# Six quads instead of four begin the MLP's first product with their plain products, and the activation sums are made in the order in which they are used

## The chip, the cores and the metric

The kernel runs on one core of one Trainium2 chip, as one launch. The metric is device microseconds of that core. Before the change the median of 3 runs is 2004.18 us (2002.26 to 2006.55). The engines are named as the profile names them: PE is TensorE's matmul, PEld its weight load, DVE is VectorE, ACT is ScalarE, POOL is GpSimd (it issues the stores), SP is SyncE (it issues the weight loads).

## The reference

Two layers of a decoder trunk on 1024 tokens of width 1024, in float32. Each layer is a mixer and then a squared-ReLU MLP, both with a norm ahead and a norm behind. Only the MLP matters here:

```
def squared_relu_mlp(h, w1, w2):
    return jnp.square(jax.nn.relu(h @ w1)) @ w2
...
        y = squared_relu_mlp(rms_norm(h, g[2]), ffn_w1[layer], ffn_w2[layer])
        h = h + rms_norm(y, g[3])
```

`w1` is 1024 x 4096 and `w2` is 4096 x 1024, for each of the two layers.

## The kernel before, in words

**Numbers.** Each float32 operand is split in a high and a low part: `split_slot` (L613) lets ACT cast to the high part (L614) and DVE subtract it from the source for the low part (L615). `mm3` issues three matmuls (L237 high by high, L238 high by low, L239 low by high).

**Quads.** The MLP's first product (`mlp_up`, L729) is cut into 16 quads of 256 hidden columns. A quad is a 2 x 2 block product (two halves of the contraction, two halves of the tokens) done with seven products instead of eight, on sums and differences of the blocks. Every product is 12 matmuls of 128x128 by 128x512 (`prod1`, L709). `plain(q)` makes two of them from the raw weights and raw activations (splits `b11`, `b21`): the first into bank pA, which ACT copies out as `p1` into half of the slot `x0` (L750), the second into bank pB, to which DVE adds `p1` (L755). Then come p6, p5, p7, p4, p3: p6 goes on accumulating on the first product in pA with `t2`, p5 starts bank pC with `t1`, p7 goes on in pA with `t3`, p4 in pA with `t4`, p3 in pC with `b22`. ACT copies pA to `u` after p6 and after p7 (`copy_u`, L737). Bank pA is held from `plain` to p4. There are eight banks.

**Operands of a quad.** `raw_w1` loads two 512 KB pieces r0 and r1 on SP (L604 is in `load`). `w1_plain` splits r0 for `plain`; `w1_sums` makes the weight sums va and vb with four DVE instructions (L653 to L656); `w1_split` splits them into w1hsa/w1sa (for p5 and p7) and w1hsb/w1sb (for p6 and p3); `w1_a22` splits half of r1 into w1x (for p4). The activations' sums are made once for each layer: `x_sums` (L685) makes t3, t1 and t2 (each two DVE subtractions of 128x1024, L693), splits t2, t1, t3, makes t4 and splits it, and splits b22 (each split two ACT casts and two DVE subtractions).

**Start of the stage.** When the first half of the tokens is ready, `plain(0)` to `plain(3)` run (EARLY = 4); for quads 1 to 3 r0 is loaded ahead into a slot of its own (`early_load`) and again with r1 later (`raw_w1`). When the second half is ready, `x_sums` is called as a whole, then `w1_split(0, "a")`, `w1_a22(0)`, and the rest of quad 0. The loop over q then does quad q's p4 and p3 and quad q+1's p6, p5 and p7; from quad 4 on it also does `plain(q+1)` ahead of p4(q), and p6(q+1) comes behind p3(q) instead of ahead of p4(q).

**Order.** The written order gives the priority; the order on each engine is fixed when the program is built, by priority among the instructions that are then reckoned to be ready. Each engine works through its list in that order. On-chip tiles come from 50 slots of 128x1024 float32 (`NSLOT`, `Slots`): `get` takes the slot that was freed longest ago, and a new tile waits for the last reader of the old one, which can be a store's landing. `sums(q)` makes the seven operands of the second product from quad q and stores them with POOL (L810, L811); their slots come back two to three products later in the written order.

Of the kernel before, what the change touches and what calls it, by code (L numbers as in the profile page):

```python
# [19 lines left out]
P = 128  # L20
# [129 lines left out]
class Trunk:  # L150
# [463 lines left out]
        self.nc.scalar.copy(hi, src)  # L614
        self.nc.vector.tensor_tensor(lo, src, hi.bitcast(F32), op=ALU.subtract)  # L615

    EARLY = 4

    def early(self, layer, step):

# [62 lines left out]
        return self.x_split([self.xr[dh, 0, j] for j in range(2)], True)  # L683

    def x_sums(self):  # L685
        tt = self.nc.vector.tensor_tensor
        b = {(dh, tg): [self.xr.pop((dh, tg, j)) for j in range(2)] for dh in range(2) for tg in range(2)}
        t1, t2, t4, b22 = b[0, 1], b[0, 0], b[1, 0], b[1, 1]
        t3 = [self.slots.get([P, 2, 512], F32, "t3") for _ in range(2)]

        def sub(d, x, y):
            for j in range(2):
                tt(d[j].t, x[j].t, y[j].t, op=ALU.subtract)  # L693
        sub(t3, b22, t1)
        sub(t1, t1, t2)
        sub(t2, b22, t1)
        self.xb["t2"] = self.x_split(t2, True)
        self.xb["t1"] = self.x_split(t1)
        self.xb["t3"] = self.x_split(t3)
        sub(t4, t4, t2)  # L700
        for s in t2:
            s.put()
        self.xb["t4"] = self.x_split(t4)
        self.xb["b22"] = self.x_split(b22)

    def mlp(self, layer, hsrc, hdst):
        self.mlp_up(layer).run(hsrc, hdst)
# [21 lines left out]
    def mlp_up(self, layer):  # L729
        nc, sl = self.nc, self.slots  # L730
        NQ, EARLY = 16, self.EARLY
        tt = nc.vector.tensor_tensor
        self.xb = {}
        Q = [dict() for _ in range(NQ)]

        def copy_u(q, j, bank):
            nc.scalar.copy(Q[q]["u"].t[:, j, :], bank.t)  # L737

        def relu2(ap, src):
            nc.scalar.activation(ap, src, AF.Relu)  # L740
            nc.scalar.activation(ap, ap, AF.Square)  # L741

        def plain(q):

            d = Q[q]
            d["A"] = self.hold("pA")
            d["x0"] = sl.get([P, 2, 512], F32, "hx0")
            c11, p1 = d["x0"].t[:, 0, :], d["x0"].t[:, 1, :]
            self.prod1(d["A"], q, "0", 0, "b11", True)
            nc.scalar.copy(p1, d["A"].t)  # L750
            b = self.hold("pB")
            self.prod1(b, q, "0", 1, "b21", True)
            for n in ("h0", "l0"):
                self.w1q[q][n].put()
            tt(c11, b.t, p1, op=ALU.add)  # L755
            b.put()
            relu2(c11, c11)

        def p6(q):
            Q[q]["u"] = sl.get([P, 2, 512], F32, "u")  # L760
            self.prod1(Q[q]["A"], q, "sb", 0, "t2", False)
            copy_u(q, 1, Q[q]["A"])

        def p5(q):
            Q[q]["C"] = self.hold("pC")
            self.prod1(Q[q]["C"], q, "sa", 1, "t1", True)

        def p7(q):
            d = Q[q]
            self.prod1(d["A"], q, "sa", 0, "t3", False)  # L770
            for n in ("sa", "hsa"):
                self.w1q[q][n].put()
            copy_u(q, 0, d["A"])
            d["x1"] = sl.get([P, 2, 512], F32, "hx1")
            c22 = d["x1"].t[:, 1, :]
            tt(c22, d["C"].t, d["u"].t[:, 0, :], op=ALU.add)
            relu2(c22, c22)

        def p4(q):
            d = Q[q]  # L780
            self.prod1(d["A"], q, "x", 0, "t4", False)
            self.w1q[q]["x"].put()
            relu2(d["x0"].t[:, 1, :], d["A"].t)
            d["A"].put()

        def p3(q):
            d = Q[q]
            self.prod1(d["C"], q, "sb", 1, "b22", False)
            for n in ("sb", "hsb"):
                self.w1q[q][n].put()  # L790
            c12 = d["x1"].t[:, 0, :]
            tt(c12, d["C"].t, d["u"].t[:, 1, :], op=ALU.add)  # L792
            d["C"].put()
            relu2(c12, c12)

        def sums(q):

            d = Q[q]
            g, r = q // 4, slice((q % 4) * 512, (q % 4) * 512 + 512)
            a11, a12 = d["x0"].t[:, 0, :], d["x0"].t[:, 1, :]  # L800
            a21, a22 = d["x1"].t[:, 0, :], d["x1"].t[:, 1, :]
            d["x2"] = sl.get([P, 2, 512], F32, "hx2")
            s1, s2 = d["x2"].t[:, 0, :], d["x2"].t[:, 1, :]
            tt(s1, a21, a22, op=ALU.add)
            tt(s2, s1, a11, op=ALU.subtract)
            tt(a21, a11, a21, op=ALU.subtract)
            tt(d["u"].t[:, 1, :], a12, s2, op=ALU.subtract)
            hs = self.hs[layer]
            for n, j in (("x0", 0), ("x1", 2), ("x2", 4)):
                nc.gpsimd.dma_start(hs[j:j + 2, g, :, r].rearrange("j p f -> p j f"), d[n].t)  # L810
            nc.gpsimd.dma_start(hs[6, g, :, r], d["u"].t[:, 1, :])  # L811
            self.later(8.0, lambda: [d[n].put() for n in ("x0", "x1", "x2", "u")])


        self.wait(lambda: self.xready[0] == [True, True])
        self.xb["b11"] = self.x_plain(0)
        self.xb["b21"] = self.x_plain(1)
        plain(0)
        self.early_load(layer, 2)
        self.early_load(layer, 3)  # L820
        plain(1)
        self.w1_sums(0)
        self.early_plain(2)
        plain(2)
        self.w1_split(0, "b")
        self.early_plain(3)
        plain(3)
        self.wait(lambda: self.xready[1] == [True, True])
        self.xready = [[False, False], [False, False]]
        self.gpost.put()  # L830
        self.x_sums()
        self.w1_split(0, "a")
        self.w1_a22(0)
        self.w1q[1]["raw"] = self.raw_w1(layer, 1)
        p6(0)
        p5(0)
        self.w1_sums(1)
        self.w1_split(1, "b")
        self.w1q[2]["raw"] = self.raw_w1(layer, 2)
        p7(0)  # L840
        down = None
        for q in range(NQ):
            n = q + 1
            if n < NQ:
                if n > 1:
                    self.w1_sums(n)
                if n >= EARLY:
                    plain(n)
                if n > 1:
                    self.w1_split(n, "b")  # L850
                if n < EARLY:
                    p6(n)
            else:
                down.step(4)
            p4(q)
            if n < NQ:
                self.w1_split(n, "a")
            else:
                down.step(4)
            p3(q)  # L860
            if n < NQ:
                if n >= EARLY:
                    p6(n)
                if n + 2 < NQ:
                    if "raw" not in self.w1q[n + 2]:
                        self.w1q[n + 2]["raw"] = self.raw_w1(layer, n + 2)
                self.w1_a22(n)
                p5(n)
                sums(q)
                if n + 1 < NQ and n + 1 >= EARLY:  # L870
                    self.w1_plain(n + 1)
                p7(n)
                if n == NQ - 2:
                    down = Down(self, layer)
                    down.load_w(0, 11)
                    down.load_h(0)
                if n == NQ - 1:
                    down.load_w(0, 22)
                    down.load_w(0, 12)
                    down.start()  # L880
                    down.load_h(1)
            else:
                sums(q)
        return down
# [343 lines left out]
class Down:  # L1228
# [29 lines left out]
    def tt(self, dst, a, b, op):  # L1258
        return [lambda j=j: self.k.nc.vector.tensor_tensor(dst[j].t, a[j].t, b[j].t, op=op) for j in range(2)]
# [254 lines left out]
```

## Time and profile before

| what | value |
|---|---|
| median of 3 runs | 2004.18 us |
| the profiled execution's own time | 2004.15 us |
| its span in the profile | 2002.4 us |
| granted TensorE clock, mean | 0.989 |
| busy: PE, PEld, DVE, ACT, POOL | 97%, 79%, 65%, 48%, 11% |
| bytes moved by DMA | 267.74 MB |

The profile's page gives busy time and share for each engine, the span in 40 slices, the DMA queues, the chain of work that ended last, groups of instructions and DMA issues. The timeline lists the instructions of one engine in order of time, each with its start, its duration and, in brackets, the idle time ahead of it and what ended that. Matmuls are pipelined, so a row's duration (0.39 us) is longer than the distance from one start to the next; distances between starts are what counts for PE.

### The profile page before, as it was taken

The page shows a single profiled execution, that of the slowest core. Times are in us where ns is not written, and L with a number is a line of the kernel's source. Part 1 is how long each engine was busy: PE and PEld are TensorE (multiplying, and loading weights), DVE is VectorE, ACT ScalarE, POOL GpSimd, SP SyncE. Part 2 cuts the span into 40 slices and gives each one's busy share as a digit, 9 for nine tenths or more (in the row PEclk, how much of TensorE's full clock was granted, in tenths as well). Part 3 has the DMA queues.
Part 4 walks back from the last instruction along what each step waited for, and adds up shares of the span by engine and source line. Part 5 has one row for each costly group of instructions (what it writes and reads, how often), then busy time and mean ns, then how long its engine had stood idle before and what let it go on. Part 6 is the DMA issues. An engine that isn't in the chain of part 4 may idle for free.

```text
span 2002.4 us, 23647 instructions
## 1 busy us (share of the span) xinstructions
PE 1948.1 (97%) x8836; PEld 1591.2 (79%) x8836; DVE 1310.5 (65%) x2023; ACT 965.0 (48%) x1612; POOL 216.2 (11%) x327
## 2 busy tenths in 40 slices
PE   8999989999999999989999999998999999999997
PEld 6888868788878888878778778786888887888886
DVE  5664486665584787993455556658665557578798
ACT  7223464555574433464344444656555556543342
POOL 3101101111110000051000001120111111000002
PEclk9999989999999999999999999999999999999999
DMA  8114226656684535452111113322555558453444
GB/s 295 40 64 137 79 90 174 153 147 163 166 264 154 167 119 167 157 182 69 43 43 43 32 32 106 121 90 84 169 156 158 153 166 260 149 176 127 150 134 168
DMA packets 76435, 267.74 MB, mean 134 GB/s; under 512 B 9157, under 2 KB 9157, under 8 KB 76320
## 3 DMA queue, kind: packets, MB, share of 16 engines
q1 hardware_dynamic: 48240, 168.84, 25.2%
q0 software_dynamic: 26784, 95.26, 16.4%
q10 hardware_dynamic: 1296, 2.13, 0.3%
q8 instruction: 69, 1.13, 0.2%
q14 instruction: 46, 0.38, 0.1%
HBM read 187.82 MB, written 78.38 MB: 133 GB/s over the span
## 4 chain that ended last, share of the span: by engine, by line
PE 83%; issue 10%; DVE 2%; DMA 2%; POOL 1%; ACT 1%; SPq 0%; POOLq 0%; DVEq 0%; ACTq 0%
PE p L237 10%; PE p L239 10%; PE p L238 10%; PE pA L237 4%; PE pA L239 4%; PE pA L238 4%; PE op L237 3%; PE op L239 3%; PE op L238 3%; PE pC L239 2%; PE pC L238 2%; PE pC L237 2%; PE pv L1188 1%; PE s L1121 1%; PE pB L239 1%
## 5 line engine op out<-in xcount | busy, mean ns | idle before, releaser
L238 PE MATMUL p<-wl,hh 128*128 128x512 f32 x896 | 348.5, 389 | 0.5 <-DVE wl L615 0.5
L239 PE MATMUL p<-wh,hl 128*128 128x512 f32 x896 | 348.7, 389 | 0.0
L237 PE MATMUL p<-wh,hh 128*128 128x512 f32 x896 | 347.6, 389 | 0.0
L238 PEld LDWEIGHTS p<-wl,hh 128*128 128x128 f32 x896 | 168.2, 188 | 35.8 <-DVE wl L615 0.9
L237 PEld LDWEIGHTS p<-wh,hh 128*128 128x128 f32 x896 | 168.2, 188 | 34.9
L239 PEld LDWEIGHTS p<-wh,hl 128*128 128x128 f32 x896 | 168.2, 188 | 34.9
L614 ACT CAST hh<-hr 128x1024 fp32r<-128x1024 f32 x112 | 115.2, 1052 | 123.5 <-PE p L239 41.2
L615 DVE TENSOR_TENSOR hl<-hr,hh 128x1024 fp32r<-128x1024 f32 x112 | 134.2, 1218 | 44.0 <-ACT hh L614 19.9
L1380 DVE TENSOR_TENSOR acc<-acc,p 128x512 f32<-128x512 f32 x168 | 114.4, 681 | 41.9 <-PE p L239 40.5
L810 POOL DMA_DIRECT2D hs<-hx x96 | 69.2, 722 | 568.5 <-ACT hx L741 417.3
L740 ACT ACTIVATE hx<-hx 128x512 f32<-128x512 f32 x96 | 60.6, 631 | 118.3 <-DVE hx L755 55.1
L614 ACT CAST wh<-w2r 128x1024 fp32r<-128x1024 f32 x64 | 67.0, 1053 | 95.4 <-PE p L238 90.3
L114 DVE TENSOR_TENSOR wlo<-raw,whi 128x1024 fp32r<-128x1024 f32 (+1 forms) x57 | 68.2, 1201 | 47.3 <-ACT whi L113 30.3
L615 DVE TENSOR_TENSOR wl<-w2r,wh 128x1024 fp32r<-128x1024 f32 x64 | 77.7, 1218 | 32.6 <-ACT wh L614 32.6
L1157 ACT ACTIVATE e<-s,nm 128x512 f32<-128x512 f32 (+3 forms) x96 | 54.6, 579 | 63.7 <-DVE nm L1150 54.0
L113 ACT CAST whi<-raw 128x1024 fp32r<-128x1024 f32 (+1 forms) x57 | 58.6, 1037 | 52.2 <-PE pp L239 15.8
L741 ACT ACTIVATE hx<-hx 128x512 f32<-128x512 f32 x128 | 80.9, 632 | 3.5
L614 ACT CAST wh<-t 128x1024 fp32r<-128x1024 f32 x48 | 50.1, 1050 | 56.5 <-PE p L238 52.2
L792 DVE TENSOR_TENSOR hx<-pC,u 128x512 f32<-128x512 f32 x32 | 22.0, 688 | 69.5 <-PE pC L239 69.5
L615 DVE TENSOR_TENSOR w1sb<-w1vb,w1hsb 128x1024 fp32r<-128x1024 f32 x32 | 39.1, 1223 | 41.9 <-PE pA L239 40.4
L239 PE MATMUL pC<-xb,w1sa 128*128 128x512 f32 x128 | 52.0, 407 | 14.3 <-DVE w1sa L615 14.3
L211 POOL DMA_DIRECT2D gain<-in_norm_g_dram x4 | 2.3, 573 | 577.2 <-PE p L239 476.2
(313 smaller groups left out, 4911.2 us busy)
## 6 DMA issues: line engine op xcount, KB each, us to landing
hr<-hs SPq DMA_DIRECT2D x112, 512.0 KB, 5.3
hs<-hx POOLq DMA_DIRECT2D x96, 512.0 KB, 4.7
w1r<-in_w_dram SPq DMA_DIRECT2D x70, 512.0 KB, 4.1
w2r<-in_w_dram SPq DMA_DIRECT2D x64, 512.0 KB, 5.5
h<-hd POOLq DMA_DIRECT2D x24, 512.0 KB, 4.8
hd<-y POOLq DMA_DIRECT2D x20, 512.0 KB, 3.0
hs<-u POOLq DMA_DIRECT2D x32, 256.0 KB, 7.5
rx<-in_xT_dram SPq DMA_DIRECT2D x16, 256.0 KB, 7.0
```

What stands on the lines that cost most here:

```text
L113: k.nc.scalar.copy(u.hi.t[:, f], u.raw.t[:, f])
L114: k.nc.vector.tensor_tensor(u.lo.t[:, f], u.raw.t[:, f], u.hi.t[:, f].bitcast(F32), op=ALU.subtract)
L237: mm(ps, ah, bh, start=start, stop=False, skip_group_check=more)
L238: mm(ps, ah, bl, start=False, stop=False, skip_group_check=more)
L239: mm(ps, al, bh, start=False, stop=stop, skip_group_check=more)
L614: self.nc.scalar.copy(hi, src)
L615: self.nc.vector.tensor_tensor(lo, src, hi.bitcast(F32), op=ALU.subtract)
L740: nc.scalar.activation(ap, src, AF.Relu)
L741: nc.scalar.activation(ap, ap, AF.Square)
L810: nc.gpsimd.dma_start(hs[j:j + 2, g, :, r].rearrange("j p f -> p j f"), d[n].t)
L1157: nc.scalar.activation(e[m][:, kb * 512:kb * 512 + n], banks[m, kb][:, :n], AF.Exp, scale=SCALE, bias=nm[:, m:m + 1], accum_out=sm[:, kb * ...
L1380: nc.vector.tensor_tensor(o, o, bank.t, op=ALU.add)
```

## The change

Six quads are early instead of four (`EARLY, HELD = 6, 4`). For quads 4 and 5 bank pA is given back after `p1` was copied out, and is filled again later by `refill`: one matmul into a new bank, whose result is then overwritten by an ACT copy of `p1` from `x0`, after which p6 accumulates on it. `refill(4)` stands in the loop at q = 2 and `refill(5)` at q = 3. `x_sums` becomes a generator with five stops: t2, t1 and t3 are split ahead of p6(0) and p5(0), interleaved with `w1_split(0, "a")`; t4 is made and split ahead of p4(0); b22 is split ahead of p3(0). `w1_a22(0)` moves behind p5(0). Quads 4 and 5 get early loads of r0 like quads 1 to 3.

```diff
-    EARLY = 4
+    EARLY, HELD = 6, 4
...
     def x_sums(self):
...
         self.xb["t2"] = self.x_split(t2, True)
+        yield
         self.xb["t1"] = self.x_split(t1)
+        yield
         self.xb["t3"] = self.x_split(t3)
+        yield
         sub(t4, t4, t2)
         for s in t2:
             s.put()
         self.xb["t4"] = self.x_split(t4)
+        yield
         self.xb["b22"] = self.x_split(b22)
+        yield
...
         def plain(q):
             d = Q[q]
-            d["A"] = self.hold("pA")
+            a = self.hold("pA")
             d["x0"] = sl.get([P, 2, 512], F32, "hx0")
             c11, p1 = d["x0"].t[:, 0, :], d["x0"].t[:, 1, :]
-            self.prod1(d["A"], q, "0", 0, "b11", True)
-            nc.scalar.copy(p1, d["A"].t)
+            self.prod1(a, q, "0", 0, "b11", True)
+            nc.scalar.copy(p1, a.t)
+            if EARLY > q >= self.HELD:
+                a.put()
+            else:
+                d["A"] = a
...
+        def refill(q):
+
+            d = Q[q]
+            d["A"] = self.hold("pA")
+            x = self.xb["b11"][0][0].t[:, 0, :]
+            nc.tensor.matmul(d["A"].t, x[:, :P], x, start=True, stop=True)
+            nc.scalar.copy(d["A"].t, d["x0"].t[:, 1, :])
...
-        self.early_plain(2)
-        plain(2)
-        self.w1_split(0, "b")
-        self.early_plain(3)
-        plain(3)
+        for q in range(2, EARLY):
+            self.early_plain(q)
+            plain(q)
+            if q == 2:
+                self.w1_split(0, "b")
+            if q + 2 < EARLY:
+                self.early_load(layer, q + 2)
         self.wait(lambda: self.xready[1] == [True, True])
...
-        self.x_sums()
+        xs = self.x_sums()
+        next(xs)
         self.w1_split(0, "a")
-        self.w1_a22(0)
+        next(xs)
         self.w1q[1]["raw"] = self.raw_w1(layer, 1)
         p6(0)
+        next(xs)
         p5(0)
+        self.w1_a22(0)
         self.w1_sums(1)
         self.w1_split(1, "b")
...
                 if n < EARLY:
                     p6(n)
+                if self.HELD <= n + 1 < EARLY:
+                    refill(n + 1)
+                if q == 0:
+                    next(xs)
...
             p4(q)
             if n < NQ:
                 self.w1_split(n, "a")
+                if q == 0:
+                    next(xs)
```

## Rows read from the trace of the kernel before

**Rows 1.** The page: busy time of PE, and the chain that ended last by engine.

```profile
PE 1948.1 (97%) x8836; PEld 1591.2 (79%) x8836; DVE 1310.5 (65%) x2023; ACT 965.0 (48%) x1612; POOL 216.2 (11%) x327
PE 83%; issue 10%; DVE 2%; DMA 2%; POOL 1%; ACT 1%; SPq 0%; POOLq 0%; DVEq 0%; ACTq 0%
```

**Rows 2.** The waits of PE over the whole span: who waited for whom, us in total, times, longest.

```profile
PE pC L239 <- DVE w1sa L615: 14.3, 2, 7.2
PE pA L237 <- ACT u L737: 9.6, 8, 2.5
...
PE pA L238 <- DVE xb L615: 3.2, 2, 1.6
```

**Rows 3.** The timeline of PE in layer 0, from the last matmul of `plain(3)` to the first of p4(0). The first of p6(1) starts at 296.26, the first of p4(0) at 298.98, twelve matmuls later.

```profile
274.84 0.39 PE L239 MATMUL pB<-xb,w1l 128*128 128x512 f32 x1
275.58 0.50 PE L237 MATMUL pA<-xb,w1hsb 128*128 128x512 f32 x1 [0.35 <-ACT xb L614]
...
278.13 0.50 PE L238 MATMUL pA<-xb,w1hsb 128*128 128x512 f32 x1 [1.58 <-DVE xb L615]
...
281.59 0.50 PE L237 MATMUL pA<-xb,w1hsa 128*128 128x512 f32 x1 [0.68 <-ACT u L737]
...
289.49 0.80 PE L239 MATMUL pC<-xb,w1sa 128*128 128x512 f32 x1 [7.16 <-DVE w1sa L615]
...
296.26 0.39 PE L237 MATMUL pA<-xb,w1hsb 128*128 128x512 f32 x1
...
298.98 0.39 PE L237 MATMUL pA<-xb,w1x 128*128 128x512 f32 x1
```

**Rows 4.** The same of layer 1: the last matmul of `plain(3)`, the end of the longest wait, the first matmul of p6(1).

```profile
1384.04 0.39 PE L239 MATMUL pB<-xb,w1l 128*128 128x512 f32 x1
...
1398.22 0.80 PE L239 MATMUL pC<-xb,w1sa 128*128 128x512 f32 x1 [7.17 <-DVE w1sa L615]
...
1405.28 0.39 PE L237 MATMUL pA<-xb,w1hsb 128*128 128x512 f32 x1
```

**Rows 5.** Windows of 5 us in layer 0: busy time of PE, PEld, DVE, ACT and POOL, then the granted TensorE clock, the mean busy share of the DMA engines and GB/s.

```profile
275.00:280.00 5.00, 3.07 (x13) 2.06 (x12) 5.00 (x6) 3.24 (x5) 0.00 (x0) 1.00 0.35 108
280.00:285.00 5.00, 1.65 (x7) 0.71 (x5) 5.00 (x6) 2.68 (x3) 0.00 (x0) 0.87 0.00 0
285.00:290.00 5.00, 0.51 (x1) 0.50 (x2) 5.00 (x6) 0.00 (x0) 0.00 (x0) 0.50 0.53 146
290.00:295.00 5.00, 5.00 (x15) 3.87 (x14) 4.96 (x8) 2.09 (x2) 0.00 (x0) 0.60 0.44 159
...
310.00:315.00 5.00, 4.98 (x23) 3.75 (x22) 3.72 (x6) 3.73 (x6) 0.42 (x1) 1.00 1.03 224
```

**Rows 6.** The timeline of DVE in layer 0, from the gap ahead of the activation sums to w1x of quad 0; a row can merge several instructions of one kind (x2, x4).

```profile
262.70 0.69 DVE L755 TENSOR_TENSOR hx<-pB,hx 128x512 f32<-128x512 f32 x1 [2.63 <-ACT hx L750]
...
266.59 2.35 DVE L693 TENSOR_TENSOR t<-xr,xr 128x1024 f32<-128x1024 f32 x2
268.86 2.35 DVE L693 TENSOR_TENSOR xr<-xr,xr 128x1024 f32<-128x1024 f32 x2
271.13 0.68 DVE L755 TENSOR_TENSOR hx<-pB,hx 128x512 f32<-128x512 f32 x1
271.73 2.35 DVE L693 TENSOR_TENSOR xr<-xr,xr 128x1024 f32<-128x1024 f32 x2
274.00 2.35 DVE L615 TENSOR_TENSOR xb<-xr,xb 128x1024 fp32r<-128x1024 f32 x2
...
276.87 2.35 DVE L615 TENSOR_TENSOR xb<-xr,xb 128x1024 fp32r<-128x1024 f32 x2
279.13 2.35 DVE L615 TENSOR_TENSOR xb<-t,xb 128x1024 fp32r<-128x1024 f32 x2
281.40 2.35 DVE L693 TENSOR_TENSOR xr<-xr,xr 128x1024 f32<-128x1024 f32 x2
283.68 4.62 DVE L615 TENSOR_TENSOR xb<-xr,xb 128x1024 fp32r<-128x1024 f32 x4
288.22 1.22 DVE L615 TENSOR_TENSOR w1sa<-w1va,w1hsa 128x1024 fp32r<-128x1024 f32 x1
289.35 0.68 DVE L615 TENSOR_TENSOR w1x<-w1r,w1x 128x512 fp32r<-128x512 f32 x1
```

**Rows 7.** ACT: the copy of pA to `u` after p6(0) and a cast of a weight sum, from the timeline; then, of the instructions on `hx` over the whole span, the copies from PSUM to SBUF (L750) and the squares from SBUF to SBUF (L741): count, ns min/median/max, first and last start.

```profile
280.95 0.59 ACT L737 COPY u<-pA 128x512 f32<-128x512 f32 x1 [2.68 <-PE pA L239]
291.27 1.04 ACT L614 CAST w1hsa<-w1va 128x1024 fp32r<-128x1024 f32 x1 [6.44 <-DVE w1va L656]
...
L741 ACT ACTIVATE hx<-hx x128: 615/632/637, 261.6 to 1689.3; 128x512 f32<-128x512 f32 x128
...
L750 ACT COPY hx<-pA x32: 561/589/590, 254.5 to 1660.9; 128x512 f32<-128x512 f32 x32
```

**Rows 8.** DMA: the issues of the w1 loads by the page (KB each, median us to landing), and the landing of the seven stores of `u` between 240 and 420 us.

```profile
w1r<-in_w_dram SPq DMA_DIRECT2D x70, 512.0 KB, 4.1
...
DMA to landing us min/median/max: 6.8/7.7/8.4
```

**Rows 9.** The waits of DVE over the whole span: the low split of the early weights waiting for a store of `u` to land (us in total, times, longest).

```profile
DVE w1l L615 <- DMA hs<-u: 19.3, 18, 4.1
```

**Rows 10.** The timeline of PE: the first matmul of p7(4) in layer 0.

```profile
356.08 0.50 PE L237 MATMUL pA<-xb,w1hsa 128*128 128x512 f32 x1 [2.05 <-ACT u L737]
```

## Prediction

> **What bounds the kernel.** I read the page first: PE is busy 97% of the span and PE rows make 83% of the chain that ended last [rows 1]. So only what takes time from PE counts, and the next view is PE's own waits. The longest by far is a product on pC that waits for w1sa of DVE, twice, 7.2 us at most [rows 2]: once for each layer, at the place that the change touches. The third view is PE's timeline there. In layer 0 the last matmul of plain(3) starts at 274.84; twelve matmuls take 2.72 us (296.26 to 298.98), so one takes 0.227 and the next product could have started at 275.07 [rows 3]. The first of p6(1) starts at 296.26. Between them lie p6(0), p5(0) and p7(0), 36 matmuls or 8.16 us; 296.26 - 275.07 - 8.16 = 13.03 us are lost. In layer 1 it is 1384.27 to 1405.28, so 12.85 us [rows 4]. Together **25.88 us**, 1.3% of the run.
>
> What ends these waits is read from DVE's timeline [rows 6]. From 266.59 DVE has no gap: t3, t1 and t2 are made, and then all the splits of t1, t2, t3, t4 and b22 until 288.2, and only then the low half of w1sa(0) at 288.22, for which p5(0) stands 7.16 us [rows 3]. t4 and b22, 6.8 us of DVE (281.40 to 288.22), are needed only by p4(0) and p3(0), two and three products later. A part of the loss is the clock: 20 matmuls lie between 289.49 and 296.26 and take 6.77 us where 4.53 is normal, so 2.24 us; the granted clock is 0.50 in the window with the long wait and 0.60 in the next, which is the lower level of 1.2 GHz mixed with the upper of 2.4 [rows 3, 5].
>
> **The change, part by part.**
>
> Plain products of quads 4 and 5. They go from the loop to the place of the wait: 48 matmuls, 10.88 us, so p6(0) comes at 285.95, not 275.07, in layer 0. PE's sum stays the same. What now must be ready, and when (one product is 2.72): t2 at 285.95, t1 and w1sa(0) at 288.7, t3 at 291.4, w1sb(1) at 294.1, t4 and w1x(0) at 296.8, b22 at 299.6.
>
> DVE up to p4(0), from the starts in [rows 6] (1.135 for 128x1024, 0.60 for 128x512): three sums 6.81; L755 of quads 2 to 5, 2.40; splits of t2, t1, t3, 6.81; w1sa(0) 1.13; w1x(0) 0.60; the four sums for quad 1, 2.40; w1sb(1) 1.13; t4 made and split 4.54; the combine at p7(0) 0.60; the two low splits for plain(4) and (5), 2.27 if they don't fit into the gap of 2.63 ahead of 262.70. Sum 28.7, so DVE is through at 295.3 where 296.8 is asked; b22 and w1sa(1) make 298.7 where 299.6 is asked. Within this t2 ends before 280 and w1sa(0) and t1 before 283. So the wait for w1sa(0) goes altogether; the margin at p4(0) is 1.5 us and thin. I take 25.88 us as the gain, since with it also the low clock goes; the lower bound comes below.
>
> Loads. Two more of 512 KB per layer, on SP ahead of raw_w1(1), in slots whose readers are matmuls of the output projection, over when plain(0) begins. A load lands after 4.1 us [rows 8], and plain(4) starts at 275.07: hidden. raw_w1(1) waits behind them and for slots that plain(2) frees 5.44 us (plain(3)) before 275.07; its sums are needed some 15 us later. If that cover went, each load would cost its 4.1.
>
> ACT. The casts for plain(4) and (5), their copies of pA and their squares move ahead with them; ACT stood idle for 6.44 us there, until 291.27 [rows 7], so they cost nothing.
>
> refill. Four matmuls in all on PE: 0.227 each, 0.91; the first matmul after a pause has rows of 0.50 [rows 3], so at most 2. Four ACT copies from SBUF to PSUM, a form that the trace lacks: between 0.56 (a copy the other way, L750) and 0.64 (a square in SBUF, L741) [rows 7]; I take 0.63. The copy has four products, 10.9 us, until p6 needs it. Hidden; without the cover 0.63 plus its wait, as after 281.59, about 1.
>
> Slots. I followed the gets and puts of the code. Two x0 slots more are held, so the fewest free falls from two to none at p4(1). The old tile under a new one is then often a very recent one: w1hsb(2) and w1sb(2) get the slots of w1sa(1) and w1hsa(1), which p7(1) reads until just before p6(2); w1sb(3) gets that of w1sa(2), read until p7(2) ends. So p6(2) can't follow p7(1) at once. Either p4(1) goes first, after the copy of pA to `u`, for which [rows 3] show a loss of 0.83 and a slow second matmul, 0.94; or PE stands for the cast and the low split, 1.04 + 1.22 + 0.3 = 2.6 less two matmuls, about 2.1. I take 0.94, as ACT has the copy first in written order. p6(3) waits for the low split after two matmuls: 1.22 + 0.2 - 0.45, about 1.0 (0 if p4(2) fills it). For p6(5) the sums come into slots of quad 2's stores: u(2) lands 6.8 to 8.4 us after its issue [rows 8], and then two sums, a cast and a split, 4.0 us, end about when p6(5) is due: 0 to 2, I take 0.5. Together 2.44 per layer, **4.9**.
>
> POOL. Stores of quads 2 to 4 come at the spacing of a quad without plain products (five products, 13.6 us) instead of 19.0. That means two loads of 512 KB and seven stores of 256 KB, 2.75 MB, in 13.6 us, 202 GB/s; the DMA engines are full in one window of this kind even now [rows 5]. No instruction is added on POOL.
>
> The wait of 2.05 us ahead of p7(4) [rows 10] belongs to the first quad with the late order. That is now quad 6; I count neither gain nor loss, and a gain of 0 to 2 as its bounds.
>
> Sum: -25.88 + 0.91 + 4.9 = -20.1. The profiled execution took 2004.15, so **1984.1 us**; the median is 2004.18, so nothing is added for that. With the best ends: 25.88 - 0.91 - 1.9 (p6(2) alone) + 2 = 25.1, or 1979. With the worst: 25.88 - 2 - 2 x (2.1 + 1.2 + 2) = 13.3, or 1991.
>
> **A rule against it.** The window with the wait of 1.58 us was granted 1.00, the next, with the 0.68 and the first part of the 7.16, 0.87, and only the one with the rest of the long wait 0.50 [rows 3, 5]. If each of the three new short waits per layer brought a stretch of low clock like the one seen (2.24), that would be 13.4 us and the run 1997.5. The Trainium skill, "TensorE: Matmul & The Clock Gate", section "A second HAM failure mode: psum-queue depth-cycling", says that pauses between groups of matmuls as banks are cycled are enough to make the clock swing; the rows here speak against it for waits of this length.
>
> **Rivals.**
>
> 1. The wait moves on: DVE's order still puts b22 or w1sa(1) ahead of t4, or p4(0) and p3(0) find their parts late. For it: 1.5 us of margin, and an order in which DVE took t1's split before t2's (the split of 274.00 did not release p6(0), that of 276.87 did [rows 3, 6]). Against it: t4 and b22 now stand later in written order. Price 2 to 8 us per layer, say 5: 1994. Chance 0.12.
> 2. Slower, by stores. With no slot free, DVE and ACT stand in order behind a landing of `u` in each of quads 2 to 5, where no plain product covers them. Such a wait exists now, 4.1 us at the longest, 19.3 in 18 [rows 9]. If PE lost 4.1 in all four quads of both layers, 33 us: 1984.1 + 33 = 2017. It decides from 3 us per quad on ((20.1 + 4) / 8). Against it: the reuse lies 13 us or more behind the issue, and landings take 8. Chance 0.06.
> 3. The change doesn't do what it says: the early operands of quads 4 and 5 come late (slots, or their place in ACT's and DVE's lists), so PE stands before plain(4) about as long as now before p5(0). Loss 11 of 13 per layer again: about 2002. Chance 0.06.
> 4. The clock, as above: 1997.5. Chance 0.03.
>
> **How the numbers follow.** Forecast 0.73; with rivals 1 and 4 that is 0.88 faster. A difference under 0.2% (4 us) can't be told from none: rival 3, 0.06. Slower: rival 2, 0.06. The predicted time is the forecast's, 1984. The range runs from 1977, the best ends less 2 for the spread of runs (2002.26 to 2006.55), to 1995, over the worst ends and the middle of rival 1; it leaves out some 2 in 10.
>
> **What the next profile would show.** Right: PE's waits have no w1sa row of 7 us; the granted clock stays at 1.00 through the start of both up stages; p6(0) follows plain(5) at once; between p7(1) and p6(2), and at p6(3), waits of about 1 us show w1hsb or w1sb with PE as the releaser. One product to the next, plain(4) to p6(1) takes 19 us. Wrong: a wait of PE over 2 us at p4(0), p3(0) or plain(4) (rivals 1, 3); ACT or DVE rows that wait for "DMA hs" with PE idle beside them in quads 2 to 5 (rival 2); windows with a granted clock under 0.9 (rival 4).

## The result and the profile after

| | before | after |
|---|---|---|
| time, median (runs) | 2003.38 us (2002.26 to 2006.55) | 1988.06 us (1986.78 to 1993.42) |
| ratio after / before | | 0.9931, 95% 0.9917 to 0.9944 |
| profiled execution: own time, span | 2004.15, 2002.4 | 1993.42, 1991.6 |
| up stage, layer 0 and 1, together | 327.54 + 325.29 = 652.8 | 319.09 + 320.09 = 639.2 |

The changed kernel is faster by 13.8 us (11.2 to 16.6) by the ratio; the two medians differ by 15.3. The profiled execution is the slowest of its four, so it is read by stages and not by its sum. The windows view, cut where the up stages begin and end, is the first to read. Its columns are the window with its length, then the busy time of PE, PEld, DVE, ACT and POOL, the granted clock, the DMA share and GB/s. Of the kernel before:

```profile
251.54:579.08 327.54, 312.69 (x1368) 256.10 (x1367) 213.18 (x273) 179.77 (x264) 44.04 (x64) 0.98 0.58 158
579.08:1360.73 781.65, 773.11 (x3650) 628.32 (x3649) 507.83 (x994) 369.32 (x737) 76.33 (x118) 0.99 0.31 106
1360.73:1686.02 325.29, 312.70 (x1369) 256.43 (x1368) 212.06 (x271) 179.94 (x265) 42.81 (x64) 0.98 0.53 162
```

and the same cut of the changed one:

```profile
250.36:569.45 319.09, 312.27 (x1370) 256.18 (x1369) 212.22 (x273) 179.75 (x266) 44.10 (x64) 0.99 0.61 165
569.45:1355.18 785.73, 776.72 (x3651) 631.08 (x3650) 508.27 (x994) 369.49 (x737) 76.37 (x118) 0.99 0.31 106
1355.18:1675.27 320.09, 312.87 (x1371) 255.96 (x1369) 211.97 (x271) 179.25 (x267) 42.88 (x64) 0.99 0.55 169
```

The two stages that the change touches are 8.45 and 5.20 us shorter, 13.6 together. The stretch between them has the same work in both kernels and is 4.1 us longer here; over all the profiles of this study it varies from 781.0 to 785.9. The time at the lower granted clock in it goes from 3.4 to 17.0 us; it is 10.2 in the profile of before and 17.0 here. So a single profile says nothing about a few microseconds of the whole. A stage can be compared more closely, as long as its own low clock is counted apart.

The page answers to [rows 1]. PE's share of the chain fell from 83% to 74%, though PE is as busy as before. What it lost there went to "issue", time in which an engine waited for nothing that the profile shows (10% to 17%), and to POOL (1% to 3%).

```profile
PE 1951.9 (98%) x8840; PEld 1593.6 (80%) x8840; DVE 1309.8 (66%) x2023; ACT 964.9 (48%) x1616; POOL 216.4 (11%) x327
PE 74%; issue 17%; DVE 3%; POOL 3%; DMA 2%; ACT 1%; SPq 0%; POOLq 0%; DVEq 0%; ACTq 0%
```

PE's waits over the whole span answer to [rows 2] (columns as there):

```profile
PE pA L237 <- ACT u L743: 10.8, 10, 2.2
...
PE pA L239 <- DVE w1sb L615: 2.6, 2, 1.6
...
PE pC L239 <- DVE w1sa L615: 0.6, 2, 0.5
```

The row of 14.3 us on w1sa is down to 0.6, and the row on xb is gone from the top. A new row on w1sb stands there, 2.6 us. PE's timeline answers to [rows 3] and goes on past the place where those rows end:

```profile
284.54 0.39 PE L239 MATMUL pB<-xb,w1l 128*128 128x512 f32 x1
284.77 0.39 PE L237 MATMUL pA<-xb,w1hsb 128*128 128x512 f32 x1
...
306.30 0.39 PE L239 MATMUL pA<-xb,w1sa 128*128 128x512 f32 x1
306.53 0.61 PE L774 MATMUL pA<-xb 128*128 128x512 f32 x2
307.37 0.50 PE L237 MATMUL pA<-xb,w1x 128*128 128x512 f32 x1 [0.22 <-ACT u L743]
...
316.76 0.50 PE L239 MATMUL pC<-xb,w1sa 128*128 128x512 f32 x1 [0.47 <-DVE w1sa L615]
...
338.08 0.50 PE L239 MATMUL pA<-xb,w1sb 128*128 128x512 f32 x1 [1.64 <-DVE w1sb L615]
...
383.39 0.50 PE L237 MATMUL pA<-xb,w1hsa 128*128 128x512 f32 x1 [1.91 <-ACT u L743]
...
1487.07 0.50 PE L237 MATMUL pA<-xb,w1hsa 128*128 128x512 f32 x1 [1.77 <-ACT u L743]
...
1496.82 0.50 PE L237 MATMUL pA<-xb,w1x 128*128 128x512 f32 x1 [1.28 <-ACT u L743]
```

284.54 to 284.77 is the last matmul of plain(5) and the first of p6(0): one pitch, no wait. No wait follows until 306.5. After that come waits of 0.5 to 2 us: p5(2) at 316.76, p6(4) at 338.08, p7(6) at 383.39 and 1487.07, p4(6) at 1496.82. All but one are new. The one at 383.39 is the wait that stood ahead of p7(4) [rows 10]; in layer 1 that wait was only 0.24 us.

To compare kernels I add up PE's loss in an up stage: the distance from one matmul's start to the next less 0.227, wherever it is over 0.30. The loss of the first 52 us of a stage (up to about p4(1)) is "start", the rest "later". Waits and matmuls slowed by low clock both count. The medians come from three sessions, in which the kernel before has 2003.38, 2002.57 and 2002.50, so kernels are compared by their ratios. Both layers together:

| kernel | start | later | up stages | time, median | ratio to before, 95% |
|---|---|---|---|---|---|
| before | 25.8 | 10.5 | 652.8 | 2003.38 | 1 |
| changed | 0.2 | 21.5 | 639.2 | 1988.06 | 0.9931 (0.9917 to 0.9944) |
| e1 order alone | 12.8 | 13.9 | 643.2 | 1991.12 | 0.9939 (0.9925 to 0.9953) |
| e2 six alone | 1.7 | 21.1 | 640.6 | 1991.77 | 0.9943 (0.9929 to 0.9958) |
| e3 five, held | 1.0 | 18.3 | 635.8 | 1984.12 | 0.9903 (0.9888 to 0.9918) |
| e4 changed, slots of sums | 0.2 | 17.0 | 635.0 | 1984.52 (one run) | none |
| e5 changed, slots of sums and weights | 0.2 | 13.3 | 631.3 | 1981.84 | 0.9889 (0.9873 to 0.9904) |
| e6 before, slots | 25.6 | 9.6 | 651.5 | 2000.75 | 0.9990 (0.9978 to 1.0003) |
| e7 five, held, slots | 1.0 | 9.6 | 627.4 | 1977.46 | 0.9868 (0.9847 to 0.9889) |
| e8 six, held, slots | 0.2 | 14.6 | 631.5 | 1982.15 | 0.9890 (0.9869 to 0.9912) |

The changed kernel won the whole of the start, 25.6 us, and gave back 11.0 later, and 0.9 for four more matmuls: 13.7, which is what its stages are shorter by. The experiments ask two things: which part of the change won the start, and what takes the 11.0.

### The profile page after: what moved, and what is told of

It reads as the page before. It is cut to its first block, busy times and chain, and to the rows that moved or that the text cites. A ratio compares the mean times of both kernels' runs of the same rounds, so it can differ in the third digit from the quotient of the medians.

```text
span 1991.6 us, 23687 instructions
## 1 busy us (share of the span) xinstructions
PE 1951.9 (98%) x8840; PEld 1593.6 (80%) x8840; DVE 1309.8 (66%) x2023; ACT 964.9 (48%) x1616; POOL 216.4 (11%) x327
## 3 DMA queue, kind: packets, MB, share of 16 engines
q1 hardware_dynamic: 48816, 170.94, 25.6%
## 4 chain that ended last, share of the span: by engine, by line
PE 74%; issue 17%; DVE 3%; POOL 3%; DMA 2%; ACT 1%; SPq 0%; POOLq 0%; DVEq 0%; ACTq 0%
PE p L237 10%; PE p L239 10%; PE p L238 10%; PE op L237 3%; PE op L239 3%; PE op L238 3%; PE pA L237 2%; PE pA L238 2%; PE pA L239 2%; POOL hs L828 1%; PE pv L1217 1%; PE pC L237 1%; PE pC L239 1%; PE s L1150 1%; PE pC L238 1%
## 5 line engine op out<-in xcount | busy, mean ns | idle before, releaser
L615 DVE TENSOR_TENSOR hl<-hr,hh 128x1024 fp32r<-128x1024 f32 x112 | 134.5, 1220 | 44.7 <-ACT hh L614 21.5
L615 DVE TENSOR_TENSOR wl<-t,wh 128x1024 fp32r<-128x1024 f32 x48 | 58.5, 1221 | 8.6 <-ACT wh L614 8.6
L614 ACT CAST w1h<-w1r 128x1024 fp32r<-128x1024 f32 x32 | 33.5, 1051 | 57.0 <-DMA hs<-hx 44.2
```

## The experiments

**Order alone.** Four early quads as before, the sums and splits in order of use. It tells whether the two more plain products were needed at all.

```
-    EARLY, HELD = 6, 4
+    EARLY, HELD = 4, 4
```

> Four quads stay early (no refill, no extra loads); only the order of the activation sums is that of the change. Theory: cover and order each remove about half of the 26 us, and overlap. By DVE's starts p6(0) still waits about 3 us for t2, p5(0) about 0.5, p4(0) about 2.4 for t4, so some 6 of 13 us per layer stay: about 1989, no refill and nothing given back in quads 2 to 6. Rival 'the plain products are all of it': about 2003, w1sa or t2 still 7 us late. Rival 'the order is all of it': 1984 or less, start waits under 1 us.

Measured: 1991.12 us, ratio 0.9939. Half of the start's loss stays, 12.8 of 25.8. That is the forecast amount at other places: p6(0) and p5(0) hardly wait. PE's timeline of this kernel in layer 0:

```profile
284.52 0.47 PE L237 MATMUL pC<-xb,w1hsb 128*128 128x512 f32 x1 [2.40 <-ACT xb L614]
...
285.41 0.50 PE L237 MATMUL pA<-xb,w1hsb 128*128 128x512 f32 x1 [0.42 <-ACT w1hsb L614]
...
286.87 0.51 PE L237 MATMUL pA<-xb,w1x 128*128 128x512 f32 x1 [0.73 <-ACT xb L614]
```

The 7.16 us for w1sa are gone, and PE waits in pieces instead: at p3(0) for a cast of b22, at p6(1) for one of the weight sum, at p4(0) for one of t4, all by ACT. Behind them comes a stretch of low clock that costs about 1.6 us per layer. The order takes away the work that nobody needed yet; the rest is real and needs cover.

**Six alone.** Two more plain products and the refill, but the sums and splits in the old order.

```
-        xs = self.x_sums()
-        next(xs)
+        for _ in self.x_sums():
+            pass
         self.w1_split(0, "a")
-        next(xs)
+        self.w1_a22(0)
         self.w1q[1]["raw"] = self.raw_w1(layer, 1)
         p6(0)
-        next(xs)
         p5(0)
-        self.w1_a22(0)
...
-                if q == 0:
-                    next(xs)
```

> Six quads early with refill, but the activation sums made as a whole ahead of w1_split(0, a), as before. Theory: w1sa(0) comes at about 293 on DVE and p5(0) is due at 288.7, so about 4 us of wait per layer stay (6 if the clock falls): 6 to 8 us slower than the change, about 1995. Rival 'the plain products are all of it': 1988, no wait at p5(0). Rival 'the order is all of it': 2000 or more.

Measured: 1991.77 us, ratio 0.9943; start 1.7. PE's timeline at the place of the old wait:

```profile
289.13 0.39 PE L774 MATMUL pA<-xb 128*128 128x512 f32 x1
289.52 0.50 PE L237 MATMUL pA<-xb,w1hsa 128*128 128x512 f32 x1
...
290.38 0.50 PE L239 MATMUL pC<-xb,w1sa 128*128 128x512 f32 x1
```

The matmul on w1sa starts at 290.38. DVE began that operand at 289.11 (it takes 1.22), against 288.22 in [rows 6], though it now also makes two more low splits; they fit into the gap of 2.63 us that it had. I had expected 8 us of loss and found 1.7. So once the plain products of two more quads stand in front, the order is worth some 1.6 us at the start. In time this kernel and the changed one can't be told apart: their intervals overlap. Either part alone takes most of the gain, and the two don't add.

**Five, held.** One early product fewer, and no bank given back, so no refill.

```
-    EARLY, HELD = 6, 4
+    EARLY, HELD = 5, 5
```

> Five quads early, the fifth keeps its bank (no refill), order of the change. Theory: 5.4 us of cover leave at most 2 us per layer at p4(0); one slot less is held and one quad fewer runs without plain products, so less is given back later: 1983 to 1988. Rival 'six are needed': waits of 4 to 5 us per layer at the start, about 1993.

Measured: 1984.12 us, ratio 0.9903. The start costs 1.0 instead of 0.2, and later 3.2 less is lost. So in the profile the sixth quad buys 0.8 us and costs more than it buys. In time the intervals of the two kernels just touch (0.9888 to 0.9918 here), and the refill is gone as well; the last experiment settles it.

**What is lost later.** The two candidates were slots of SBUF, on which my sum had 4.9 us, and the refill, on which it had 0.9. In the changed kernel the timeline of DVE shows the first. In brackets is the idle time ahead of a row and what ended it:

```profile
325.04 0.69 DVE L615 TENSOR_TENSOR w1x<-w1r,w1x 128x512 fp32r<-128x512 f32 x1
331.00 0.69 DVE L653 TENSOR_TENSOR w1va<-w1r 128x512 f32<-128x512 f32 x1 [5.28 <-DMA hs<-u]
...
336.80 1.22 DVE L615 TENSOR_TENSOR w1sb<-w1vb,w1hsb 128x1024 fp32r<-128x1024 f32 x1
...
375.82 1.23 DVE L615 TENSOR_TENSOR w1l<-w1r,w1h 128x1024 fp32r<-128x1024 f32 x1 [4.13 <-DMA hs<-u]
...
377.57 0.69 DVE L765 TENSOR_TENSOR hx<-pB,hx 128x512 f32<-128x512 f32 x1
```

and the timeline of ACT what stands behind the second of these waits:

```profile
378.29 0.63 ACT L746 ACTIVATE hx<-hx 128x512 f32<-128x512 f32 x1 [5.55 <-DVE hx L765]
...
381.83 1.03 ACT L614 CAST w1hsb<-w1vb 128x1024 fp32r<-128x1024 f32 x1
382.76 0.58 ACT L743 COPY u<-pA 128x512 f32<-128x512 f32 x1
```

Read down: va(4) is to be written into the slot from which `u` of quad 1 is being stored. The store lands at 330.98, and DVE stands 5.28 us for it with everything queued behind. vb(4) and its split come late by as much, w1sb is written at 336.80, and PE starts p6(4) on it at 338.08. At 375.82 it is the low split of w1(7), in the slot of u(4). Behind that split DVE has the combine at 377.57, behind the combine ACT has a square and, last, a cast, and only then the copy at 382.76 for which p7(6) stands at 383.39. PE's row names "ACT u", but neither ACT nor the copy is slow: the cause lies three steps back, on a DMA.

DVE's waits in layer 0, 290 to 560, by sort (us in total, times, longest). My sum had none of them, only a wait for a store at p6(5) and the old one at p7(4), moved to p7(6):

```profile
DVE w1l L615 <- DMA hs<-u: 10.4, 8, 4.1
...
DVE w1va L653 <- DMA hs<-u: 5.3, 1, 5.3
...
DVE w1l L615 <- DMA hs<-hx: 3.8, 1, 3.8
...
DVE w1vb L654 <- DMA hs<-u: 2.0, 1, 2.0
```

The first sort is not new: over the whole span it is 16.1, against 19.3 in [rows 9]. New are the waits of the sums va. The whole chain behind the low split stood in the kernel before too, ahead of p7(4):

```profile
348.52 1.23 DVE L615 TENSOR_TENSOR w1l<-w1r,w1h 128x1024 fp32r<-128x1024 f32 x1 [4.09 <-DMA hs<-u]
350.98 0.63 ACT L740 ACTIVATE hx<-hx 128x512 f32<-128x512 f32 x1 [5.58 <-DVE hx L755]
```

(The first row is DVE's, the second ACT's.) p4(6) of layer 1 comes another way. There ACT itself stands for a store, of x0, x1 or x2, ahead of the cast w1h, and the copy that p4(6) waits for stands behind that cast:

```profile
1494.29 1.05 ACT L614 CAST w1h<-w1r 128x1024 fp32r<-128x1024 f32 x1 [5.11 <-DMA hs<-hx]
...
1496.18 0.58 ACT L743 COPY u<-pA 128x512 f32<-128x512 f32 x1
```

To test it I let the pool choose: a slot that a store was the last to read is given out last to a buffer that the caller marks. Nothing else in the code is changed, though the other buffers get other slots by it. In the first kernel only the sums va and vb are marked, in the second also w1h and w1l, the split of r0 for `plain`.

```
-    def get(self, shape, dtype, name):
+    def get(self, shape, dtype, name, stored=True):
...
-        i = self.free.pop(0)
+        i = self.free[0]
+        if not stored:
+            i = next((j for j in self.free if j not in self.was_stored), i)
+        self.free.remove(i)
+        self.was_stored.discard(i)
...
-            d[n] = self.slots.get([P, 1024], F32, "w1" + n)
+            d[n] = self.slots.get([P, 1024], F32, "w1" + n, False)
...
-            self.later(8.0, lambda: [d[n].put() for n in ("x0", "x1", "x2", "u")])
+            def back():
+                for n in ("x0", "x1", "x2", "u"):
+                    sl.was_stored.add(d[n].i)
+                    d[n].put()
+            self.later(8.0, back)
```

(In the second kernel the gets of "w1h0" and "w1l0" pass `False` as well. From here on lines stand five further down.)

> The change, and only the weight sums va and vb avoid slots that a store had read; w1h and w1l still take the oldest. Theory: the wait at p6(4) (1.8 and 1.1 us), which follows from va(4) behind the landing of u(1), goes; those at p7(6) and p4(6) (2.1 with the low clock, 1.9, 1.4), which follow from w1l(7) behind u(4), stay. Losses of the two up stages after their first 52 us: 21.5 us in the changed kernel, here about 17 to 19. Rival 'any spare slot will do': about 13, as with both.

Measured: one run of 1984.52, without an interval; later loss 17.0. The wait at p6(4) is gone, those at p7(6) and p4(6) stay (2.12 in layer 0; 1.05 and 1.38 in layer 1). This is its PE row of p7(6) in layer 0:

```profile
382.24 0.50 PE L242 MATMUL pA<-xb,w1hsa 128*128 128x512 f32 x1 [2.12 <-ACT u L748]
```

> The change, but the weight sums va, vb and the early splits w1h, w1l take the oldest free slot that no store had read, where there is one. Theory: the waits of the changed kernel at p6(4), p7(6) and p4(6) (1.8, 2.1, 1.1, 1.9 and 1.4 us, and a stretch at the low clock behind one) come from DVE and ACT standing in order behind a store's landing; they go, and it takes about 1980. Rival 'the DMA engines are too full, or the waits are another tile's': the same waits at other rows, 1986 to 1990.

Measured: 1981.84 us, ratio 0.9889; later loss 13.3. The waits at p7(6) and p4(6) go too. DVE's waits in the same window now begin with rows on ACT and PE, and there is no row on a store of `hs` among them:

```profile
DVE w1l L620 <- ACT w1h L619: 31.2, 9, 3.5
DVE hx L770 <- ACT hx L752: 20.2, 8, 2.5
DVE w1x L620 <- ACT w1x L619: 15.0, 11, 5.4
DVE w1sb L620 <- PE pA L244: 11.6, 8, 2.7
```

ACT's waits ahead of the cast w1h for a store of x0, x1 or x2 (44.2 us in 15 over the whole span of the changed kernel, 52.3 in 20 before) are gone too; the edit doesn't part them from DVE's. Each part of the edit takes away the waits that its slots account for. With both, 8.2 of the 11.0 us are back in the profile, among them a stretch of low clock worth about 1.5 that stood behind p7(6). In time the changed kernel's interval and this one's don't overlap (0.9917 to 0.9944, 0.9873 to 0.9904).

**The same slots on the kernel before**, to see whether that is a gain of its own.

> The kernel before, with the choice of slots for va, vb, w1h and w1l that avoids slots read by a store. Theory: the start keeps its 26 us, and only p7(4)'s wait (2.2 and 0.4) and some of the last quads go: 1 to 4 us faster than before, 1998 to 2001. Rival 'the slots are worth 7 us by themselves, whatever the change': 1995 or less.

Measured: 2000.75 us, ratio 0.9990 (0.9978 to 1.0003): at most 4.4 us, and none that can be told from nothing. The edit did what it is for: the 19.3 us of [rows 9] are gone from DVE's waits, and with them the wait at p7(4). But PE's later loss went only from 10.5 to 9.6, so PE had been covered against them, and its first two waits are the old ones:

```profile
PE pC L244 <- DVE w1sa L620: 12.7, 2, 7.2
PE pA L242 <- ACT u L742: 7.3, 8, 2.7
```

So most of what the slots cost in the changed kernel was made by the change: it pulled the cover away from waits that had been free.

**The refill.** Six early quads as in the second slot kernel, but all banks held, so nothing is refilled.

```
-    EARLY, HELD = 6, 4
+    EARLY, HELD = 6, 6
```

> Six quads early that all keep their bank pA (no refill), with the same choice of slots: against the one with refill it prices the refill. Theory: the refill's matmuls run while PE waits for the copy of pA after p7(1) anyway and its ACT copies are covered, so both take the same time within 1 us, unless two free banks are too few for pB: then waits of pA or pB on L765 or L756 at plain(5). Rival 'the refill costs 2 us or more': 1979 or less.

Measured: 1982.15 us, ratio 0.9890, beside 1981.84 and 0.9889 with the refill. The up stages take 631.5 and 631.3 us. The refill costs nothing that can be measured. PE's timeline says why. With the refill:

```profile
307.38 0.61 PE L779 MATMUL pA<-xb 128*128 128x512 f32 x2
308.22 0.50 PE L242 MATMUL pA<-xb,w1x 128*128 128x512 f32 x1 [0.22 <-ACT u L748]
```

and without:

```profile
306.55 0.50 PE L242 MATMUL pA<-xb,w1x 128*128 128x512 f32 x1 [0.68 <-ACT u L748]
```

Between p7(1) and p4(1) PE has to wait for the copy of pA anyway; the two refill matmuls of a layer run in that pause, and without them the pause is 0.68 instead of 0.22.

**Five, held, with the slots.** The experiments point to it: the third kernel's `EARLY, HELD = 5, 5` and the second slot kernel's edit.

> Five quads early, the fifth keeps its bank (no refill), with the same choice of slots. Theory: start loses about 1.0 us in both layers, the later losses fall from 18.3 to about 12: 1979 to 1982, the same as six with that choice. Rival 'six are better': 1984 or more.

Measured: 1977.46 us (1977.21 to 1978.18), ratio 0.9868 (0.9847 to 0.9889). It beats the kernel before by 26.4 us (22 to 31) and the changed one by 12.6 us (26.4 less 13.8, both by their ratios; 10.6 by the medians). I had expected the same as six with that choice. Beside six held, measured in the same session, every run is faster (1977.21 to 1978.18 against 1980.14 to 1983.55), so here the sixth quad costs more than it buys. PE's waits, whole span:

```profile
PE tp L295 <- ACT x L271: 5.5, 4, 2.9
PE pA L242 <- ACT u L748: 4.7, 4, 1.9
```

The first row is a stage that the change doesn't touch. The row on `u` is 4.7 where the changed kernel has 10.8. Start and later together lose 10.6 here, 21.7 in the changed kernel and 36.3 before.

## Why the prediction was right, and the term that was mis-sized

Predicted 1984.0 (1977 to 1995), measured 1988.06. The sign, the mechanism and the gain at the start held; what is given back is twice what I took (11.0 and 0.9 where the sum had 4.9 and 0.9), and it is lost at other places than I had.

- *The gain of 25.88.* Start loss fell from 25.8 to 0.2. p6(0) follows plain(5) at once in both layers, and the granted clock of 284.77 to 298.37 is 1.00 where [rows 5] had 0.50 and 0.60, so the 2.24 us of low clock per layer came back with the wait, as the sum had it.

```profile
284.77:298.37 13.60, 13.60 (x61) 11.26 (x60) 10.69 (x12) 9.58 (x14) 0.00 (x0) 1.00 0.10 31
```

- *DVE up to p4(0).* The margin of 1.5 us was enough. DVE went further ahead than I had it: the splits of t4 and b22 all end by 293.88, where p4(0) starts at 295.65. The two more low splits took the gap that [rows 6] show ahead of 262.70, and w1sa(0) is made before the activation sums instead of after t2.

```profile
263.60 1.22 DVE L615 TENSOR_TENSOR w1sa<-w1va,w1hsa 128x1024 fp32r<-128x1024 f32 x1
```

- *Which part does it.* The text treated order and plain products as one cause with one price. They are two: six alone leaves 1.7 of 25.8 at the start, the order alone 12.8. The prediction didn't ask this, and its number didn't need it.
- *Loads, ACT, POOL: nothing.* The loads of plain(4) and (5) made nobody late: no wait of PE stands ahead of either. Their landing is 4.2 us by the median of the page, 4.1 in [rows 8]. The 202 GB/s under "POOL" has its 2.75 MB in units of 1024 x 1024 bytes; in the units of the rate it is 212. From 306 to 381 the window shows 186.
- *The refill, 0.91.* Four matmuls were added, but in a pause (above). The copy from SBUF to PSUM takes 0.586 us (median of 4), where I took 0.63 between 0.56 and 0.64; nobody waited for it.
- **The failed step is "Slots", 4.9**, with its neighbour, "neither gain nor loss" for p7(6). The term was mis-sized: later loss rose by 11.0. By place, layer 0 and 1:

| place | taken per layer | measured |
|---|---|---|
| between p7(1) and p6(2) | 0.94 | 0.49, 0.49 |
| p5(2), for w1sa(2) | not listed | 0.74, 0.44 |
| p6(3) | 1.0 | 0.1 to 0.2 each |
| p6(4), behind the store of u(1) | 0 | 1.92, 1.20 |
| p6(5), behind the store of u(2) | 0.5 | none |
| p7(6), behind the store of u(4) | what p7(4) had: 2.32, 0.51 | 2.18, 2.05 |
| p4(6), behind a store that ACT waits for | not listed | none, 1.56 |
| low clock after a wait | 0 | 1.55, 1.71 |

The three places that the term names lost about 1.3 us, not 4.9. That the whole came out within a factor of about two, though the places were wrong, is luck.

The first and third rows, slots that PE still reads, came out smaller than forecast. In the first, the two refill matmuls fill a part of the pause; six held, without them, loses 0.95 there, as forecast. At p6(3) PE mixed the matmuls of the neighbouring products into the gap. The slots that a store still reads came out larger, and a quad earlier than I had them. I had followed the pool up to the sums of quad 5 and put the stores' wait there. The list of gets and puts of the code has it at va(4), which gets the slot of u(1): issued at 322.67, landed at 330.98, 8.3 us where [rows 8] have 6.8 to 8.4. The landing time was right. What failed is the distance: rival 2 was set aside because "the reuse lies 13 us or more behind the issue", but DVE was ready to write that slot at 325.73, 3.1 us after the issue, and the slot of u(4) at 371.69, 4.4 us after 367.26. The distance was not worked out for each get, only for those that I had picked. The wait at p7(6) was read as one that moves along with the late order, without its cause. In layer 0 it is the old one, with the same chain behind a store; in layer 1 it grew from 0.51 to 2.05. Both go with the slots, and so does p7(4)'s in the kernel before.
- *Rival 2 (slower by stores)* was right in kind. It named 3 us per quad as the point from which it decides; DVE did stand 5.28 and 4.13 us in two of the quads, but PE only about 2, since the matmuls ahead had covered the rest. I gave it 4.1 at every quad or nothing, where what happened lies between.
- *Rivals 1 and 3* did not come: no wait at p4(0) or p3(0), none ahead of plain(4). Rival 3's "about 2002" doesn't follow from its own loss: 1984.1 and 22 make 2006.
- *The signs.* Of those for "right", the waits of about 1 us on w1hsb or w1sb behind PE did not come. Of those for "wrong", two did: DVE behind "DMA hs" with PE idle in quad 4, and a window granted less than 0.9. The sum stayed in its range even so, since the gain at the start was whole.
- *Rival 4 (clock).* I let the rows of before speak against it for waits of this length, and that was too strong. After the wait of 1.91 at 383.39 came a stretch of low clock: the window 385 to 390 is granted 0.67.

```profile
380.00:385.00 5.00, 3.09 (x14) 2.25 (x13) 2.76 (x5) 3.28 (x6) 2.03 (x3) 0.99 0.35 110
385.00:390.00 5.00, 5.00 (x17) 3.97 (x16) 1.92 (x2) 2.64 (x4) 0.70 (x2) 0.67 1.06 236
390.00:395.00 5.00, 5.00 (x24) 4.14 (x23) 3.99 (x5) 2.32 (x4) 0.00 (x0) 1.00 0.63 146
```

It cost 1.55. A wait of 2.20 at 1668.09, the end of layer 1's stage, was followed by another, 1.71; the kernel before has a wait of 2.50 at that place and no low clock behind it, so this part need not be the change's. The waits of 1.64 at 338.08, 1.77 at 1487.07 and 1.28 at 1496.82 brought none. The Trainium skill, "TensorE: Matmul & The Clock Gate", section "A second HAM failure mode: psum-queue depth-cycling", tells of a kernel whose clock swings because PE pauses often between groups of matmuls. The runs here agree for some of the waits of about 2 us and not for the shorter ones, and the price was 3.3 us in all, not 13.4.

What stays open: five early quads lose 3 to 4 us less later than six, with the slots as they were (18.3 against 21.5) and with the new ones (9.6 against 13.3). With the new slots PE's waits of 0.22 at p4(1) and of 0.44 and 0.40 at p5(2) are gone, and that at the last p7 of layer 0 is 0.41 instead of 1.33. Fewer slots are held with five, but how that saves these waits was not followed get by get.

## What to carry to other kernels

Work that is moved ahead to fill a wait was covering something where it stood: list the waits that engines already have there and cost nothing, and ask of each what it costs bare. With a pool of buffers handed out in turn, work out for every get the time since its old reader, and if that reader is a store, count its landing; handing a stored buffer out last is an edit of a few lines, and it was worth nothing that can be told before the change and 6 to 8 us after (by medians 1988.06 to 1981.84, by ratios 0.9931 to 0.9889). Fill a wait with as little as closes it: the fifth early quad was worth more than the fifth and sixth together (1977.46 against 1982.15, new slots and no refill in both).

## What the runs showed of the hardware

- The same length of wait can and can't bring the lower clock: after 1.91 us of idle PE at 383.39 in the changed kernel the granted clock fell for 3.4 us, after 2.12 at 382.24 in the first slot kernel it stayed at 1.00, as it did in the kernel before after the 2.05 of [rows 10].
- A stage that no edit touches differs by up to 4.9 us from one profile to the next (781.0 to 785.9 us), and the two longest (785.7 and 785.9) have the most time at the lower clock, 17.0 us.
- ACT writes 128x512 fp32 from SBUF into PSUM in 0.586 us, about as long as the other way (0.589 in [rows 7]).
